# Four of eight row tiles transposed by VectorE in 32 by 32 blocks and two passes through memory

## The chip, the cores and the metric

The kernel runs on one core of a Trainium2 chip. A core has TensorE (matrix products, written PE in the profile), VectorE (DVE), ScalarE (ACT), GpSimd (POOL) and SyncE (SP), which issues most of the DMAs. Each runs its own instructions in order and waits for others by semaphores. SBUF is the working memory with 128 partitions; PSUM, eight banks of 128 x 512 float32, takes the matrix products. The metric is device time in microseconds, the median of several runs.

## The reference

One decoder layer on x of 1024 rows by 1024 columns, all in float32:

```python
h = rms_norm(x, norm_mix_g)
u = h @ w_in                                  # 1024 x 3328, split in five
y_pool = pool_mixer(u_pool, pool_w, pool_scale)
y_hgrn = hgrn2_mixer(q_raw, f_raw, i_raw, g_raw, lb, hgrn_norm_g)   # 6 heads
x = x + concat([y_pool, y_hgrn]) @ w_out
h2 = rms_norm(x, norm_mlp_g)
x = x + square(relu(h2 @ w_up)) @ w_down      # 1024 x 4096 and back
return rms_norm(x, final_norm_g)
```

The change lies between `w_out` and `w_up`, where h2 is made. A product on TensorE sums over the partitions of its operands. h2 comes out of the row norm with its rows on the partitions, and `h2 @ w_up` sums over its columns, so h2 has to be transposed.

## The kernel before

Rows are worked in NT = 8 tiles of P = 128 and columns in halves of 512. A float32 product is made of three: each operand is split into a high part, the value rounded to a shorter float (a cast on ScalarE, L126), and a low part, the rest (a subtraction on VectorE, L127). `mm3` (L132 to L134) then adds high by high, high by low and low by high. An operand is usable when both casts are done, and each split costs ScalarE and VectorE a pass over the data.

The stage around the change has these steps.

1. `product_out(i, 0)` makes the left half of x + mix @ w_out for tile i, 24 matmuls into one PSUM bank, for all eight tiles. `rows_out` adds x on VectorE (L828), squares on ScalarE with a sum (L880), and stores the half row with POOL's DMA (L881).
2. Then for each tile: the other half of its row of x is loaded by SP (L938), `product_out(i, 1)` makes the right half, and `rows_normed(i)` scales the row by 1/rms and the gain into `hn` (L887; the power is POOL's, L869).
3. `mlp_input(i - 1)` follows: eight transposes of 128 x 128 on TensorE (L893) into two banks, and two copies on ScalarE (L895) into `quad`. It runs one tile behind, so that TensorE need not wait for the norm. `quad[dh, h]` holds columns half dh (on the partitions, four blocks) of rows half h, 512 rows. Tiles 0 to 3 fill the two quarters `quad[0, 0]` and `quad[1, 0]`, tiles 4 to 7 the others.
4. `w_up` is multiplied by a seven-product scheme (Strassen-like): sums and differences of the quarters of h2 and of the weights go into products numbered 1 to 7. Operands 1 and 2 are the quarters of tiles 0 to 3, split in full after tile 4's product (`operand`). `mixed_blocks(i)` makes, for each of tiles 4 to 7, its part of operand 5 and the differences that become operands 6, 3, 7 and 4.
5. `up_product(n)` is 24 matmuls into two banks. Up group 0 has the order 1, 2, 5, 6, 3, 7, 4; the later groups start 1, 5, 6. Weights are loaded by SP (L958), summed or subtracted on VectorE, and split into `whi_wu` and `wlo_wu`.

On TensorE the order is that of the program. In front of up group 0, from `in_order.__enter__()` until the last operand of the group is made, it is written out for VectorE and ScalarE as well. Elsewhere a planner orders these two engines and SP by when it expects each instruction to be ready and by the place in the program. TensorE's order here is: right-half products 0 and 1, transposes of tile 0, product 2, transposes of tile 1, and so on to transposes of tile 6, up product 1, transposes of tile 7, up products 2, 5, 6, 3, 7, 4.

The pool `wsplit` has four buffers of each of two tags, `whi` and `wlo`. At the time of the change they pass from the four blocks of the left half of w_out to `hn_0`, `hn_1` and the x halves `xr_0`, `xr_1`, and to the first up weights.

The heads before this stage already use the helpers that the change calls. `blocks_turned` (L157) is one VectorE instruction that transposes each 32 x 32 block of a tile in place of the whole. `blocks_moved` writes the result to memory (L164) and reads it back in four DMAs (L167), one for each 32 partitions, so that every block lands on its partitions.

Of the kernel before, what the change touches and what calls it, by code (L numbers as in the profile page):

```python
# [10 lines left out]
F32 = mybir.dt.float32  # L11
# [6 lines left out]
P = 128  # L18
# [3 lines left out]
KT = D // P  # L22
# [43 lines left out]
def kernel(  # L66
# [20 lines left out]
    pe, act, dve, pool = nc.tensor, nc.scalar, nc.vector, nc.gpsimd  # L87
# [13 lines left out]
    def spill(shape, name):  # L101
        return dram.tile(shape, F32, name=name, tag=name)
# [50 lines left out]
    B = 32  # L153

    def blocks_turned(dst, src):

        dve.transpose(dst, src.rearrange("p n (b i) -> p b n i", i=B))  # L157

    def blocks_moved(dst, src, name):


        n = src.shape[2] * B
        t = spill([P, 4 * n], name)
        nc.sync.dma_start(t, src.rearrange("p b n i -> p (b n i)"))  # L164
        tv = t.rearrange("(a j) (b x) -> b j a x", a=4, b=4)
        for b in range(4):
            nc.sync.dma_start(dst[b * B:(b + 1) * B], tv[b])  # L167
# [7 lines left out]
    wring = {"raw": [], "split": [], "n": 0}  # L175
# [28 lines left out]
    with ExitStack() as pa:  # L204
# [474 lines left out]
        with tc.manual_schedule(engines={mybir.EngineType.PE, mybir.EngineType.DVE, mybir.EngineType.Activation}):  # L679
            for j in load_xt(0, (("Q", 2), ("Q", 2), ("K", 2), ("K", 2))):  # L680
# [5 lines left out]
                n = 1 if j < 2 else 2 if j % 2 == 0 else 0  # L686
# [103 lines left out]
        def bank(name):  # L790
            return psb.tile([P, 512], F32, tag="bank", name=name)
# [27 lines left out]
    def pair_of(pool_, name):  # L819

        t = pool_.tile([P, 2, 4, 512], F32R, tag="big", name=name)
        return t[:, 0], t[:, 1]
# [14 lines left out]
    with ExitStack() as pb:  # L837
# [4 lines left out]
        for n, (pool_, tag) in enumerate(((rawp, "raw"), (rawp, "raw"), (sums, "sum"), (sums, "sum"))):  # L842
            t = pool_.tile([P, 2, 512], F32, tag=tag, name=f"xl_{n}")
# [29 lines left out]
        quad = {k: quadp.tile([P, 4, 512], F32, tag="quad", name=f"quad_{k[0]}{k[1]}") for k in ((0, 1), (1, 0), (0, 0), (1, 1))}  # L873
# [9 lines left out]
        def rows_normed(i):  # L883
            r = rstd_of_parts([sss[i][:, e:e + 1] for e in range(2)], f"n2_{i}")
            for dh in range(2):
                cs = slice(dh * 512, (dh + 1) * 512)
                dve.scalar_tensor_tensor(out=hns[i][:, cs], in0=xs[i, dh], scalar=r, in1=g2[:, cs], op0=ALU.mult, op1=ALU.mult)  # L887

        def mlp_input(i):
            for dh in range(2):  # L890
                pt = bank(f"pt_h2_{i}_{dh}")
                for j in range(4):
                    pe.transpose(pt[:, j * P:(j + 1) * P], hns[i][:, (4 * dh + j) * P:(4 * dh + j + 1) * P], ident)  # L893
                c = i % 4 * P
                act.copy(quad[dh, i // 4][:, :, c:c + P], pt.rearrange("p (j t) -> p j t", j=4))  # L895
# [3 lines left out]
        def operand(n, pool_, src):  # L899
            h2[n] = pair_of(pool_, f"h2op_{n}")  # L900
            split(*h2[n], src)
# [7 lines left out]
        def mixed_blocks(i, between=lambda: None):  # L909


            b11, b12, b21, b22 = (quad[k][:, :, i % 4 * P:(i % 4 + 1) * P] for k in ((0, 0), (0, 1), (1, 0), (1, 1)))
            sub(b11, b12, b11)
            part = *(t[:, :, i % 4 * P:(i % 4 + 1) * P] for t in h2[5]), b11
            hi_part(*part)
            between()
            lo_part(*part)
            sub(b11, b22, b11)
            sub(b12, b22, b12)
            sub(b21, b21, b11)  # L920

        def product_out(i, dh):
            ps = bank(f"ps_o_{dh}_{i}")
            products_out({i: ps}, right_weight if dh else left_weight, MIX_ORDER)
            rows_out(i, dh, ps)
# [3 lines left out]
        for i in range(2, NT):  # L929
            product_out(i, 0)  # L930

        his = [wring["split"][0].tile([P, D], F32, tag="whi", name=f"hn_{n}") for n in range(2)]
        los = [wring["split"][0].tile([P, 2, 512], F32, tag="wlo", name=f"xr_{n}") for n in range(2)]
        hns = {i: his[i % 2] for i in range(NT)}
        for i in range(NT):
            xs[i, 1] = los[i % 4 // 2][:, i % 2]
        for i in range(NT):
            nc.sync.dma_start(xs[i, 1], x[0, i * P:(i + 1) * P, 512:])  # L938
            product_out(i, 1)
            rows_normed(i)  # L940
            if i:
                mlp_input(i - 1)
            if i == 4:
                operand(1, big, quad[0, 0])
                operand(2, big, quad[1, 0])
                h2[5] = pair_of(big2, "h2op_5")
            if i > 4:
                mixed_blocks(i - 1)
# [73 lines left out]
        for _ in up_product(1, split_first[1], first["a"], True):  # L1022
            pass
        mlp_input(7)
        made = {}
        mixed_blocks(7, lambda: made.update({6: first_weights(6)}))
# [121 lines left out]
    with ExitStack() as pd:  # L1148
# [116 lines left out]
        for at, (g, n) in enumerate(products[:-2]):  # L1265
            last = g == DOWN_GROUPS - 1
            pools, a, b = ahead
# [12 lines left out]
        with tc.manual_schedule(engines={mybir.EngineType.DVE, mybir.EngineType.Activation, mybir.EngineType.Pool}):  # L1280
            pools, a, b = ahead
# [84 lines left out]
```

## Time and profile before

| | |
|---|---|
| median of 3 runs | 1070.4 us (1070.05 to 1071.48) |
| the profiled execution | 1070.01 us |
| its span | 1068.2 us, 14588 instructions |
| DMA | 142.82 MB, mean 134 GB/s |

The span is the time from the first to the last instruction in the trace; all times of instructions count from its start. A timeline line has the start, the time, the engine, the line of the program, the operation, out<-in and the shapes, and in brackets how long the engine stood idle before and what released it. A matmul line's time includes the depth of TensorE's pipeline; the distance of two starts is what it takes. In the summary of one tile, three numbers with slashes are the shortest, the median and the longest time of an instruction, in ns.

### The profile page before, as it was taken

To read this page: it belongs to the slowest core of one execution; us is meant where nothing else is said; L and a number is where in the kernel's file an instruction comes from. 1 tells how busy PE (TensorE), PEld (TensorE's weight loads), DVE (VectorE), ACT (ScalarE), POOL (GpSimd) and SP (SyncE) were. 2 spreads that over 40 slices of the span, in tenths; PEclk is the share of its full clock that TensorE was granted. 3 is DMA by queue.
4 is the path that set the end of the run, shared out by engine and by line. 5 is a ranking of instruction groups with operands and counts; after the bars stand their busy time and mean duration, and the time that the engine had idled before them with its cause. 6 is when DMAs were issued, how large, how long until landed. Compare 5 with 4: busy or idle time off the path is not lost.

```text
span 1068.2 us, 14588 instructions
## 1 busy us (share of the span) xinstructions
PE 1056.5 (99%) x5890; PEld 885.5 (83%) x5890; DVE 748.0 (70%) x932; ACT 446.5 (42%) x720; POOL 78.3 (7%) x126
## 2 busy tenths in 40 slices
PE   9999999999999899999999999999999999999997
PEld 8988889988888688888888888888888888888886
DVE  5377686176588824798855865775979878777775
ACT  5856544354544523463223223323435242423334
POOL 0001000001000111101101100100100000000001
PEclk9999999999999999999999999999999999999999
DMA  9521121131111723225435434428983344254104
GB/s 307 176 61 55 56 70 40 59 93 49 39 40 41 246 104 114 70 99 179 174 104 193 178 109 148 178 99 323 375 344 119 116 160 175 101 202 153 39 1 158
DMA packets 74116, 142.82 MB, mean 134 GB/s; under 512 B 5440, under 2 KB 47168, under 8 KB 70464
## 3 DMA queue, kind: packets, MB, share of 16 engines
q1 hardware_dynamic: 63408, 106.32, 29.3%
q0 software_dynamic: 9344, 33.56, 8.0%
q10 hardware_dynamic: 1296, 2.00, 0.5%
q8 instruction: 46, 0.75, 0.3%
q14 instruction: 22, 0.18, 0.1%
HBM read 101.49 MB, written 40.37 MB: 133 GB/s over the span
## 4 chain that ended last, share of the span: by engine, by line
PE 96%; DVE 3%; issue 0%; POOL 0%; ACT 0%; POOLq 0%
PE ps_ua L134 5%; PE ps_ua L133 5%; PE ps_ua L132 5%; PE ps_dx L132 5%; PE ps_dx L133 5%; PE ps_dx L134 5%; PE ps_v L304 3%; PE ps_dy L132 3%; PE ps_uc L134 3%; PE ps_dy L133 3%; PE ps_uc L133 3%; PE ps_uc L132 3%; PE ps_dy L134 3%; PE ps_o L134 2%; PE ps_o L132 2%; PE ps_o L133 2%
## 5 line engine op out<-in xcount | busy, mean ns | idle before, releaser
L126 ACT CAST wdop<-raw_wd 128x2048 fp32r<-128x2048 f32 x28 | 53.6, 1913 | 156.1 <-PE ps_dy L134 49.6
L132 PE MATMUL ps_ua<-h2op,whi_wu 128*128 128x512 f32 x256 | 99.7, 389 | 0.0
L134 PE MATMUL ps_ua<-h2op,wlo_wu 128*128 128x512 f32 x256 | 99.6, 389 | 0.0
L133 PE MATMUL ps_ua<-h2op,whi_wu 128*128 128x512 f32 x256 | 99.6, 389 | 0.0
L132 PE MATMUL ps_dx<-wdop,hop 128*128 128x512 f32 x252 | 98.0, 389 | 0.0
L133 PE MATMUL ps_dx<-wdop,hop 128*128 128x512 f32 x252 | 98.0, 389 | 0.0
L134 PE MATMUL ps_dx<-wdop,hop 128*128 128x512 f32 x252 | 98.0, 389 | 0.0
L127 DVE TENSOR_TENSOR wdop<-raw_wd,wdop 128x2048 fp32r<-128x2048 f32 x28 | 64.1, 2290 | 29.3 <-ACT wdop L126 29.3
L126 ACT CAST hop<-hraw 128x2048 fp32r<-128x2048 f32 x28 | 53.4, 1911 | 31.6 <-DMA hraw<-hid 19.8
L127 DVE TENSOR_TENSOR hop<-hraw,hop 128x2048 fp32r<-128x2048 f32 x28 | 63.9, 2283 | 2.5 <-ACT hop L126 2.5
L126 ACT CAST whi_wu<-wsum 128x1024 fp32r<-128x1024 f32 x22 | 23.2, 1054 | 93.6 <-DVE wsum L825 38.7
L127 DVE TENSOR_TENSOR wlo_wu<-raw_wu,whi_wu 128x1024 fp32r<-128x1024 f32 x23 | 28.0, 1221 | 47.6 <-ACT whi_wu L126 47.6
L828 DVE TENSOR_TENSOR x<-ps_dx,x 128x512 f32<-128x512 f32 x64 | 43.8, 686 | 18.7 <-PE ps_dx L134 18.7
L133 PEld LDWEIGHTS ps_ua<-h2op,whi_wu 128*128 128x128 f32 x256 | 48.1, 188 | 10.0
L132 PEld LDWEIGHTS ps_ua<-h2op,whi_wu 128*128 128x128 f32 x256 | 48.1, 188 | 10.0
L134 PEld LDWEIGHTS ps_ua<-h2op,wlo_wu 128*128 128x128 f32 x256 | 48.1, 188 | 9.9
L134 PEld LDWEIGHTS ps_dx<-wdop,hop 128*128 128x128 f32 x252 | 47.3, 188 | 9.9
L132 PEld LDWEIGHTS ps_dx<-wdop,hop 128*128 128x128 f32 x252 | 47.3, 188 | 9.8
L133 PEld LDWEIGHTS ps_dx<-wdop,hop 128*128 128x128 f32 x252 | 47.3, 188 | 9.7
L1061 POOL DMA_DIRECT2D hid<-hid x56 | 29.9, 534 | 283.9 <-DVE hid L1058 216.9
L132 PE MATMUL ps_uc<-h2op,whi_wu 128*128 128x512 f32 x128 | 49.8, 389 | 0.0
L133 PE MATMUL ps_uc<-h2op,whi_wu 128*128 128x512 f32 x128 | 49.8, 389 | 0.0
(287 smaller groups left out, 2704.7 us busy)
## 6 DMA issues: line engine op xcount, KB each, us to landing
hid<-hid POOLq DMA_DIRECT2D x56, 512.0 KB, 3.2
hraw<-hid SPq DMA_DIRECT2D x28, 1024.0 KB, 5.1
raw_wu<-in_w_up_dram SPq DMA_DIRECT2D x32, 512.0 KB, 3.8
raw_wd<-in_w_down_dram SPq DMA_DIRECT2D x16, 1024.0 KB, 7.2
xt<-in_x_t_dram SPq DMA_DIRECT2D x16, 256.0 KB, 5.5
xn<-in_x_dram SPq DMA_DIRECT2D x8, 512.0 KB, 7.0
x<-x_mid SPq DMA_DIRECT2D x8, 512.0 KB, 6.1
raw_q<-in_w_in_dram SPq DMA_DIRECT2D x6, 512.0 KB, 4.4
```

Of the source, the lines that this page charges most:

```text
L126: act.copy(hi, src)
L127: dve.tensor_tensor(out=lo, in0=src, in1=hi.bitcast(F32), op=ALU.subtract)
L132: pe.matmul(ps, lh, rh, start=start, stop=False, skip_group_check=goes_on)
L133: pe.matmul(ps, lh, rl, start=False, stop=False, skip_group_check=goes_on)
L134: pe.matmul(ps, ll, rh, start=False, stop=stop, skip_group_check=goes_on)
L304: pe.matmul(banks[i][:, :VC], hT[h][part][:, j, i * P:(i + 1) * P], w[:, b, :], start=j == 0 and part == 0 and w is wh, stop=j == KT - 1 a ...
L828: dve.tensor_tensor(out=out_, in0=a, in1=b, op=ALU.add)
L1061: nc.gpsimd.dma_start(store[n][:, at, :], t)
```

## The change

For tiles 0 to 3 (`TURNED = 4`), `mlp_input` does without TensorE. VectorE turns the 32 x 32 blocks of the normalised tile into `turned`; SP writes that to memory and reads it back into `placed` in four DMAs; two copies on ScalarE put `placed` into the same places of `quad` as before. It is called right behind `rows_normed(i)` instead of one tile later. Tiles 4 to 7 go as before. `turned` and `placed`, two buffers each, are taken from the tags `whi` and `wlo` of `wsplit`, ahead of `hn` and `xr`.

```diff
+        TURNED = 4
+
         def mlp_input(i):
+            if i < TURNED:
+                t, n = placed[i % 2], turned[i % 2]
+                blocks_turned(n, hns[i].rearrange("p (n t) -> p n t", t=P))
+                blocks_moved(t.rearrange("p a n i -> p a (n i)"), n, f"h2_{i}")
+                c = i % 4 * P
+                for dh in range(2):
+                    dst = quad[dh, i // 4][:, :, c:c + P].rearrange("p j (a i) -> p j a i", i=B)
+                    act.copy(dst, t[:, :, 4 * dh:4 * dh + 4].rearrange("p a j i -> p j a i"))
+                return
             for dh in range(2):
...
+        turned = [wring["split"][0].tile([P, 4, KT, B], F32, tag="whi", name=f"h2_turned_{n}") for n in range(2)]
+        placed = [wring["split"][0].tile([P, 4, KT, B], F32, tag="wlo", name=f"h2_placed_{n}") for n in range(2)]
         his = [wring["split"][0].tile([P, D], F32, tag="whi", name=f"hn_{n}") for n in range(2)]
...
             rows_normed(i)
-            if i:
+            if i < TURNED:
+                mlp_input(i)
+            elif i > TURNED:
                 mlp_input(i - 1)
             if i == 4:
                 operand(1, big, quad[0, 0])
```

## The prediction

> **What bounds the kernel now.** First the busy shares and the chain of work that ended last, both on the page:
>
> ```profile
> PE 1056.5 (99%) x5890; PEld 885.5 (83%) x5890; DVE 748.0 (70%) x932; ACT 446.5 (42%) x720; POOL 78.3 (7%) x126
> PEclk9999999999999999999999999999999999999999
> PE 96%; DVE 3%; issue 0%; POOL 0%; ACT 0%; POOLq 0%
> ```
>
> TensorE bounds: 99% busy, full clock, 96% of the chain. An average says little about one stage, so next the busy time by stretch (us, then PE, PEld, DVE, ACT, POOL, clock, DMA share, GB/s):
>
> ```profile
> 406.00:434.00 28.00, 28.00 (x141) 23.54 (x140) 13.06 (x26) 10.38 (x21) 5.69 (x10) 1.00 0.37 123
> 434.00:461.00 27.00, 27.00 (x135) 22.37 (x135) 25.23 (x38) 12.63 (x22) 4.16 (x6) 1.00 0.13 49
> 461.00:495.00 34.00, 34.00 (x151) 28.16 (x150) 33.93 (x32) 17.79 (x19) 3.25 (x6) 1.00 0.40 137
> ```
>
> The transposes lie at 411 to 457. TensorE never stops there. VectorE is half idle up to 434 and then has no room: 25.2 of 27 and 33.9 of 34 us. So the second question is by how much VectorE is ahead of TensorE after 434. The timelines of both engines answer it:
>
> ```profile
> 434.82 4.50 DVE L127 TENSOR_TENSOR h2op<-quad,h2op 128x2048 fp32r<-128x2048 f32 x2
> 460.57 0.69 DVE L907 TENSOR_TENSOR h2op<-quad,h2op 128x512 fp32r<-128x512 f32 x1
> 462.61 0.39 PE L132 MATMUL ps_uc<-h2op,whi_wu 128*128 128x512 f32 x1
> 476.75 1.22 DVE L907 TENSOR_TENSOR wlo_wu<-wdif,whi_wu 128x1024 fp32r<-128x1024 f32 x1
> 478.93 0.39 PE L132 MATMUL ps_ua<-h2op,whi_wu 128*128 128x512 f32 x1
> 493.90 1.21 DVE L127 TENSOR_TENSOR wlo_wu<-wsum,whi_wu 128x1024 fp32r<-128x1024 f32 x1
> 495.25 0.39 PE L132 MATMUL ps_uc<-h2op,whi_wu 128*128 128x512 f32 x1
> ```
>
> Matmuls follow each other every 0.226 us (462.61 is the first of up product 5; 24 take 5.44). A product's second matmul needs the low part of its operand, its third that of its weights, whose load starts some 0.2 earlier. Product 5 of group 0 has its operand at 461.26 and needs it at 462.83: 1.6 us to spare. Product 7 has its weights at 477.97, needs them at 479.2: 1.2. Product 5 of group 1 has them at 495.11, needs them at 495.5: **0.4 us**. VectorE works without a break between these, so the stage is balanced to 0.4 us: whatever TensorE saves before it is kept only if VectorE's row of work moves earlier too.
>
> **The change part by part.** *Removed: 32 of 64 transposes.* Their group, the chain in order of time, and the additions on VectorE that follow each product:
>
> ```profile
> L893 PE MATMUL pt_h<-ident,hn x64: 270/272/328, 411.6 to 457.0; 128*128 128x128 f32 x64
> ...
> 411.56 0.23 PE ps_o L134
> 411.79 0.87 PE pt_h L893 x8
> 412.66 0.24 PE ps_o L132
> ...
> 400.94 0.69 DVE L828 TENSOR_TENSOR xl<-ps_o,xl 128x512 f32<-128x512 f32 x1 [4.75 <-PE ps_o L134]
> 406.38 0.69 DVE L828 TENSOR_TENSOR xr<-ps_o,xr 128x512 f32<-128x512 f32 x1 [4.75 <-PE ps_o L134]
> 424.53 0.69 DVE L828 TENSOR_TENSOR xr<-ps_o,xr 128x512 f32<-128x512 f32 x1 [1.99 <-PE ps_o L134]
> 430.86 0.69 DVE L828 TENSOR_TENSOR xr<-ps_o,xr 128x512 f32<-128x512 f32 x1 [2.33 <-PE ps_o L134]
> ```
>
> The matmuls overlap, so 8 x 0.272 isn't the price. A group of eight costs 0.87 to 0.9 us: the period is 6.33 with it, 5.44 without. Four groups: **3.6 us**, the most that can be won. Product 5 would start at 459.0.
>
> *Added: block transposes, a write, four reads per tile.* The kernel does the same for five heads, so this trace has the prices; the last two lines are SP's timeline for one head:
>
> ```profile
> L157 DVE STREAM_TRANSPOSE turned<-on x5: 1237/1245/1246, 109.2 to 306.5; 128x1024 f32<-128x1024 f32 x5
> DMA to landing us min/median/max: 2.6/2.6/4.5
> L167 SPq DMA_DIRECT2D onT<-on x20: 312/425/1707, 113.1 to 313.3; - x20
> DMA to landing us min/median/max: 2.4/2.9/5.0
> ...
> 263.05 0.34 SPq L164 DMA_DIRECT2D on<-turned  x1
> 265.74 2.08 SPq L167 DMA_DIRECT2D onT<-on  x4
> ```
>
> The first landing line is of the write, the second of the reads. VectorE: 4 x 1.245 = 5.0 us, all before 428, beside 15 us of idle: no cost. ScalarE makes as many copies of 128x512 as before, now out of SBUF, where its squares of that size (first row below) take 0.63 us against a copy's 0.58: nothing. What is new there is that a copy waits for reads, with the squares of later rows behind it, and behind these their normalisation; ScalarE is free for 18 of the 28 us, so a copy that comes in time costs nothing. SP issues 20 more DMAs and stands from a write to its landing: 2.7 + 2.1 = 4.8 of 5.44 us per tile. POOL's queue gets nothing. Behind SP's waits stand the x rows and weights:
>
> ```profile
> 412.75 0.63 ACT L880 ACTIVATE junk<-xr 128x512 bf16<-128x512 f32 x1
> 396.63 14.03 SPq L938 DMA_DIRECT2D xr<-in_x_dram  x5
> 427.90 0.38 SPq L958 DMA_DIRECT2D raw_wu<-in_w_up_dram  x1
> 449.51 1.22 DVE L828 TENSOR_TENSOR wsum<-raw_wu,raw_wu 128x1024 f32<-128x1024 f32 x1
> ```
>
> Four of the five x rows are wanted before the first write is ready, and can go first; their buffers now come free at the end of the left half's last product (added at 400.94), 4 us later, which leaves 5 us before 406.38. Later rows are loaded about 10 us ahead of their product's end, these weights 21.6 us before 449.51. No cost; if one were kept behind a write, 2.7 to 4.5 us of that margin would go.
>
> *Moved: when operand 1 can be made.* It needs all four tiles in the first half of `quad`, hence the fourth tile's transfers:
>
> ```profile
> 408.84 0.75 DVE L887 SCALAR_TENSOR_TENSOR hn<-xl,rstd_n,g 128x512 f32<-128x512 f32 x1 [0.69 <-POOL rstd_n L869]
> 409.51 0.75 DVE L887 SCALAR_TENSOR_TENSOR hn<-xr,rstd_n,g 128x512 f32<-128x512 f32 x1
> 432.40 0.58 ACT L895 COPY quad<-pt_h 128x512 f32<-128x512 f32 x1
> 432.87 3.73 ACT L126 CAST h2op<-quad 128x2048 fp32r<-128x2048 f32 x2
> ```
>
> Rows are normalised 3.9 us after their addition (406.38 to 410.26). The fourth is added at 406.38 + 3 x 5.44 = 422.7, normalised at 426.6, turned at 427.85; write issue to first read 2.7: 430.6; the fourth read issued 1.3 later, landed after 2.9: 434.8; two copies 1.1, a cast 1.9: VectorE begins operand 1 at **437.9**, against 434.82, so +3.1. With both maxima (4.5 and 5.0) it is 441.9, +7.1. I take 438.5, +3.7: nearer the medians, but not on them, since 512 KB of weights (427.90) and a row of x are issued right after the normalisation, beside this write.
>
> *Moved: two weight splits.* The new tiles take two of the four `whi`/`wlo` buffers, so the first two up weights wait for the copies of the third and fourth tile:
>
> ```profile
> 415.76 2.35 DVE L127 TENSOR_TENSOR wlo_wu<-raw_wu,whi_wu 128x1024 fp32r<-128x1024 f32 x2
> ```
>
> In before they lay in idle time. The first still finds a gap (431 to 437); the second, 1.17 us, may fall into the full stretch: 0 to 1.2, I take 0.6.
>
> *What VectorE gets back.* Row 5 is added at 433.6 and normalised before 437.5, ahead of operand 1 instead of behind it: 2.1 us. And it had these waits after 434:
>
> ```profile
> 442.44 0.75 DVE L887 SCALAR_TENSOR_TENSOR hn<-xl,rstd_n,g 128x512 f32<-128x512 f32 x1 [0.46 <-POOL rstd_n L869]
> 447.58 0.75 DVE L887 SCALAR_TENSOR_TENSOR hn<-xl,rstd_n,g 128x512 f32<-128x512 f32 x1 [0.46 <-POOL rstd_n L869]
> 453.96 0.75 DVE L887 SCALAR_TENSOR_TENSOR hn<-xl,rstd_n,g 128x512 f32<-128x512 f32 x1 [0.75 <-POOL rstd_n L869]
> ```
>
> 1.7 us together; with more work queued most are filled: 0.8 to 1.7, I take 1.2.
>
> **The sum.** VectorE's row of work moves by 3.7 + 0.6 - 2.1 - 1.2 = **+1.0 us** (ends: 3.1 + 0 - 2.1 - 1.7 = -0.7; 7.1 + 1.2 - 2.7, row 6 then being ahead as well, - 0.8 = +4.8). TensorE, 3.6 us early, runs into it at products 5 and 7, and last in group 1, where 0.4 us was to spare: the end moves by +1.0 - 0.4 = **+0.6 us** (-1.1 to +4.4). The 3.6 us are won and spent waiting. The profiled execution took 1070.01 us around its span of 1068.2, against a median of 1070.4; from the median: **1071.0 us**. A measurement of this kernel can tell about 0.2%, 2.1 us, from no change.
>
> **The rivals.** *Late transfers, slower.* Same mechanism, one place: the fourth tile's write and reads. It decides once they land 2.1 us later than by the medians (after 436.9): then operand 1 begins at 440.0, the row moves by 5.2 + 0.6 - 2.1 - 1.2 = 2.5 and the end by 2.1. For it: the maxima in the landing lines, SP's 4.8 of 5.44 us, and the squares behind ScalarE's waiting copies, which would delay the next tile's write. Against: medians of five heads, and a DMA share of 0.37. It gives 1072.5 to 1074.8, about 1073.5; chance 0.33.
>
> *VectorE's row does not bind, faster.* If the order on VectorE were made anew so that arithmetic on `hid` at 481 to 495 goes behind group 1's weights, TensorE would keep most of 3.6 us: 1066.8. Against: in group 0 that order is written by hand, and there product 5's operand, now ready at 461.26, would have to be ready by 459.2, though its source comes 3.1 us later. Chance 0.13.
>
> *The clock falls.* No slice shows a lower clock in this trace, whose longest wait of TensorE is
>
> ```profile
> PE ps_o L132 <- ACT mT_hi L126: 2.7, 1, 2.7
> ```
>
> If the waits, 3.6 + 4.4 us at the far end, came as one stop and a whole product ran at half rate after it, that adds 5.4 us: 1080. Chance 0.04. The Trainium skill, "TensorE: Matmul & The Clock Gate", section "Why this matters for your kernels", warns of gaps over about 3 us, after which the clock is halved; no run here shows one so long.
>
> The Trainium skill's "VectorE: DVE Perf Modes", section "Rules for kernel authors", also speaks against the change: a 128x128 transpose belongs on TensorE where its result may go to PSUM. By it alone there would be nothing to win, 1070.4 or more. The trace agrees that the detour is long, 434.8 - 426.6 = 8.2 us for turn, write and reads where TensorE's group takes 0.9.
>
> **How the numbers follow.** Balanced, so within 0.2%: 0.50, own range 1069.3 to 1072.5; late 0.33; faster 0.13; clock 0.04. Faster 0.13, same 0.50, slower 0.37. The range 1069.0 to 1075.0 leaves out the faster case and the clock's.
>
> **What would show it.** 32 transposes in the group of L893; additions 5.44 us apart up to 433.6; operand 1 on VectorE at about 438.5; TensorE waits of some 4 us in all between 440 and 500, for VectorE's `h2op`, `hn`, `wlo_wu`. No waits there and product 5 at 459 would make it wrong, as would x rows waiting behind writes on SP.

## The result, and the profile after

The kernel after takes **1089.06 us** (median of 4 runs, 1088.48 to 1089.51) against 1070.22 us for the kernel before in the same series, 18.8 us more. The ratio on record, 1.0166 with an interval of 1.0153 to 1.0179, makes it 17.8 us, a little less than these two medians do; where ratios are compared below, the loss is counted as 18 us. It is slower, where 1071.0 was forecast and 1075.0 was the upper end. The profiled execution took 1089.51 us around a span of 1087.7. One of the six timed runs of the kernel called e11 below took 6098.79 us and is left out of its time.

The page of the kernel after: TensorE's busy time, the clock that it was granted in 40 slices, and the chain that ended last.

```profile
PE 1060.2 (97%) x5858; PEld 886.7 (82%) x5858; DVE 752.8 (69%) x936; ACT 447.6 (41%) x720; POOL 77.5 (7%) x126
PEclk9999999999999899889999999999999999999999
PE 94%; DVE 3%; ACT 1%; issue 1%; DMA 1%; POOL 0%; SPq 0%; POOLq 0%; DVEq 0%; ACTq 0%
```

TensorE has 32 instructions fewer and is busy 3.7 us *longer*, and the clock row, all nines before, has three eights, at slices 14, 17 and 18. So there are two things to look for: stops, and matmuls that run slower. The waits of TensorE between 380 and 520 (us in total, times, longest); in the kernel before this view is empty:

```profile
PE pt_h L904 <- DVE hn L887: 8.2, 1, 8.2
PE ps_ua L132 <- ACT h2op L126: 5.1, 1, 5.1
PE ps_ua L133 <- DVE h2op L127: 1.5, 1, 1.5
```

Three waits, 14.8 us: one for a normalised row, two for operand 1. The first is followed back on VectorE, whose timeline has the additions of the right halves (L828) and operand 1's low part (L127):

```profile
415.61 0.69 DVE L828 TENSOR_TENSOR xr<-ps_o,xr 128x512 f32<-128x512 f32 x1 [0.29 <-PE ps_o L134]
...
431.93 1.29 DVE L828 TENSOR_TENSOR xr<-ps_o,xr 128x512 f32<-128x512 f32 x2 [11.15 <-PE ps_o L134]
437.37 1.29 DVE L828 TENSOR_TENSOR xr<-ps_o,xr 128x512 f32<-128x512 f32 x2 [4.15 <-PE ps_o L134]
...
465.98 4.49 DVE L127 TENSOR_TENSOR h2op<-quad,h2op 128x2048 fp32r<-128x2048 f32 x2 [0.62 <-ACT h2op L126]
```

The additions of rows 0 and 1 are 5.44 us apart (410.17, 415.61); then come rows 2 and 3 together, 16.3 us later. The bracket names TensorE, but `ps_o` of row 2 had been done since about 421, so it must have been the other operand, x. Why x was late, SP's timeline tells:

```profile
400.41 14.02 SPq L952 DMA_DIRECT2D xr<-in_x_dram  x3
415.35 0.33 SPq L164 DMA_DIRECT2D h<-h_turned  x1
418.21 1.75 SPq L167 DMA_DIRECT2D h_placed<-h  x4
420.80 0.34 SPq L164 DMA_DIRECT2D h<-h_turned  x1
421.25 1.60 SPq L952 DMA_DIRECT2D xr<-in_x_dram  x1
422.90 0.43 SPq L974 DMA_DIRECT2D raw_wu<-in_w_up_dram  x1
425.10 1.75 SPq L167 DMA_DIRECT2D h_placed<-h  x4
426.94 14.38 SPq L952 DMA_DIRECT2D xr<-in_x_dram  x3
```

Three x rows are issued first (0, 1 and 4); rows 2, 3 and 6 stand in the last line, behind the write and the reads of tile 1, and are issued from 426.94 on, 6 us after row 2's product was done. The buffers would explain it: rows 2 and 3 lie in `xr_1`, and `xr_0`, `xr_1` and both `placed` have the tag `wlo`.

The clock of this stretch, by windows of 3 us (PE busy, then PEld, DVE, ACT, POOL, clock, DMA share, GB/s):

```profile
443.00:446.00 3.00, 0.52 (x3) 0.52 (x4) 3.00 (x6) 0.89 (x1) 0.54 (x1) 0.50 0.84 269
446.00:449.00 3.00, 3.00 (x12) 2.66 (x11) 2.25 (x6) 1.32 (x3) 0.55 (x1) 0.53 1.05 269
...
466.00:469.00 3.00, 1.47 (x3) 0.86 (x4) 3.00 (x2) 1.74 (x1) 0.00 (x0) 0.50 0.20 74
469.00:472.00 3.00, 3.00 (x9) 2.32 (x8) 3.00 (x4) 0.89 (x2) 0.00 (x0) 0.50 0.00 0
```

Behind each of the two stops the clock is 0.50, and TensorE goes at about half rate: behind the second one its matmuls start 0.43 us apart instead of 0.226.

```profile
469.34 0.63 PE L132 MATMUL ps_ua<-h2op,whi_wu 128*128 128x512 f32 x1
469.77 0.63 PE L133 MATMUL ps_ua<-h2op,whi_wu 128*128 128x512 f32 x1
```

### The profile page after: what moved, and what is told of

Its sections match the earlier page's. It is cut to its first block, busy times and chain, and to the rows that moved or that the text cites. A ratio compares the mean times of both kernels' runs of the same rounds, so it can differ in the third digit from the quotient of the medians.

```text
span 1087.7 us, 14558 instructions
## 1 busy us (share of the span) xinstructions
PE 1060.2 (97%) x5858; PEld 886.7 (82%) x5858; DVE 752.8 (69%) x936; ACT 447.6 (41%) x720; POOL 77.5 (7%) x126
## 4 chain that ended last, share of the span: by engine, by line
PE 94%; DVE 3%; ACT 1%; issue 1%; DMA 1%; POOL 0%; SPq 0%; POOLq 0%; DVEq 0%; ACTq 0%
PE ps_ua L133 5%; PE ps_ua L132 5%; PE ps_ua L134 5%; PE ps_dx L134 5%; PE ps_dx L133 5%; PE ps_dx L132 5%; PE ps_v L304 3%; PE ps_dy L134 3%; PE ps_uc L132 3%; PE ps_dy L133 3%; PE ps_uc L134 3%; PE ps_uc L133 3%; PE ps_dy L132 3%; PE ps_o L132 3%; PE ps_o L133 2%; PE ps_o L134 2%
## 5 line engine op out<-in xcount | busy, mean ns | idle before, releaser
L132 PE MATMUL ps_ua<-h2op,whi_wu 128*128 128x512 f32 x256 | 100.8, 394 | 5.1 <-ACT h2op L126 5.1
L133 PE MATMUL ps_ua<-h2op,whi_wu 128*128 128x512 f32 x256 | 100.7, 393 | 1.5 <-DVE h2op L127 1.5
L127 DVE TENSOR_TENSOR wdop<-raw_wd,wdop 128x2048 fp32r<-128x2048 f32 x28 | 64.1, 2290 | 27.3 <-ACT wdop L126 27.3
L127 DVE TENSOR_TENSOR hop<-hraw,hop 128x2048 fp32r<-128x2048 f32 x28 | 63.9, 2283 | 3.2 <-ACT hop L126 3.2
L127 DVE TENSOR_TENSOR wlo_wu<-raw_wu,whi_wu 128x1024 fp32r<-128x1024 f32 x23 | 28.1, 1222 | 47.7 <-ACT whi_wu L126 47.6
L828 DVE TENSOR_TENSOR x<-ps_dx,x 128x512 f32<-128x512 f32 x64 | 43.9, 687 | 18.7 <-PE ps_dx L134 18.7
```

The costliest lines, as they stand in the source:

```text
L127: dve.tensor_tensor(out=lo, in0=src, in1=hi.bitcast(F32), op=ALU.subtract)
L132: pe.matmul(ps, lh, rh, start=start, stop=False, skip_group_check=goes_on)
L133: pe.matmul(ps, lh, rl, start=False, stop=False, skip_group_check=goes_on)
L828: dve.tensor_tensor(out=out_, in0=a, in1=b, op=ALU.add)
```

## The experiments

The theory after the result: the x rows behind tile 1's reads make the first stop, operand 1 is late for a reason of its own, and each stop is paid for again by the clock. The rivals: the pass through memory, or VectorE's turns, make all of it. Ratios are to the kernel before, timed on the same chip; 1.0010 is 1.07 us.

### x rows first in the program (e1), and buffers outside the tag (e2)

e1 moves the loads of rows 0 to 3 ahead in the program and leaves the buffers:

```diff
-        for i in range(NT):
+        for i in range(4):
             nc.sync.dma_start(xs[i, 1], x[0, i * P:(i + 1) * P, 512:])
+        for i in range(NT):
+            if i >= 4:
+                nc.sync.dma_start(xs[i, 1], x[0, i * P:(i + 1) * P, 512:])
```

> The change, with the loads of the first four x rows written ahead of the loop, so that they are planned before anything asks for the buffers of the blocks read back. Theory A (the x rows of tiles 2 and 3 share a tag with those buffers and are therefore issued behind the reads of tile 1; their lateness is nearly all of the 18.8 us): 1070 to 1074, no wait of TensorE for a normalised tile over 1 us, rows 2 and 3 added within 6 us of one another. Theory B (the way through memory itself is too slow, and the rows' order only a symptom): 1083 or more, with TensorE still waiting 5 us or more for operand 1.

e2 leaves the loads where they are in the program and takes `turned` and `placed` out of the shared tags, as views of fields of `quad` that tiles 4 to 7 fill later:

```diff
-        turned = [wring["split"][0].tile([P, 4, KT, B], F32, tag="whi", name=f"h2_turned_{n}") for n in range(2)]
-        placed = [wring["split"][0].tile([P, 4, KT, B], F32, tag="wlo", name=f"h2_placed_{n}") for n in range(2)]
+        def half_of(q, n, name):
+            return q[:, 2 * n:2 * n + 2, :].rearrange("p a (b i) -> p (a b i)", i=B).rearrange("p (a n i) -> p a n i", a=4, i=B)
+        turned = [half_of(quad[1, 1], n, "t") for n in range(2)]
+        placed = [half_of(quad[0, 1], n, "p") for n in range(2)]
```

> The change, with its four buffers laid into two quarters that nothing uses before tile 4, so that no tag is shared with the x rows or the weights; the loads stay where they were. Theory A: x rows 0 to 3 are issued together, and the time is that of e1 or up to 1 us less, since the first two weight splits move back too: 1069.5 to 1073. Theory B: 1083 or more. If the shared tag is not what orders the rows, rows 2 and 3 are late here as well, and the time is near 1089.

e1: 1077.67 us, 1.0055 (1.0043 to 1.0068). e2: 1077.42 us, 1.0054 (1.0041 to 1.0068). Two different edits, the same result: two thirds of the loss, 1.1% or 12 us, is gone, and the wait for the normalised row with it. e1's waits of TensorE:

```profile
PE ps_ua L132 <- ACT h2op L126: 4.2, 1, 4.2
PE ps_ua L133 <- DVE h2op L127: 1.6, 1, 1.6
PE ps_uc L133 <- DVE h2op L918: 0.9, 1, 0.9
PE ps_ua L132 <- ACT hid L1088: 0.4, 1, 0.4
```

So the rows were behind the reads because of both: the shared tag, and their later place in the program; taking away either is enough. Neither range of the expectations was met, for both theories were too simple: a third of the loss is left. Where it lies shows e2's timeline of SP:

```profile
396.90 14.01 SPq L955 DMA_DIRECT2D xr<-in_x_dram  x5
...
424.80 0.32 SPq L164 DMA_DIRECT2D h<-quad  x1
425.17 4.54 SPq L167 DMA_DIRECT2D quad<-h  x8
429.83 0.36 SPq L164 DMA_DIRECT2D h<-quad  x1
...
435.16 1.94 SPq L167 DMA_DIRECT2D quad<-h  x4
```

and of ScalarE:

```profile
447.34 0.63 ACT L880 ACTIVATE junk<-xr 128x512 bf16<-128x512 f32 x1 [5.04 <-DVE xr L828]
...
448.44 1.14 ACT L899 COPY quad<-quad 128x512 f32<-128x512 f32 x2
449.48 3.70 ACT L126 CAST h2op<-quad 128x2048 fp32r<-128x2048 f32 x2
```

All x rows go first. But tile 3's write, issued at 429.83, has landed only at 435.16, 5.3 us later, and its reads, of which the slowest took 5.3 us, are in at about 442. The planner has put the copies behind the square of row 7, so that they run at 448.44, and operand 1's low part begins at 451.47.

### The rows alone (e3)

All eight tiles are transposed by TensorE, one tile behind as before; turns, writes and reads of the first four are issued in the changed order, and nobody uses what they bring:

```diff
-                c = i % 4 * P
-                for dh in range(2):
-                    dst = quad[dh, i // 4][:, :, c:c + P].rearrange("p j (a i) -> p j a i", i=B)
-                    act.copy(dst, t[:, :, 4 * dh:4 * dh + 4].rearrange("p a j i -> p j a i"))
                 return
+
+        def mlp_input_pe(i):
...
-            elif i > TURNED:
-                mlp_input(i - 1)
+            if i:
+                mlp_input_pe(i - 1)
```

> All eight tiles transposed on TensorE one tile behind as before, and beside that, for four tiles, the turning, the write and the four reads of the change, whose result is not used (the copies out of it are left out). Theory A: the x rows are late as in the change, TensorE waits some 8 us or more for a normalised tile, and 3.6 us are not saved: 1080 to 1092. Theory B: nothing waits for the detour, 1070 to 1073.

1082.15 us, 1.0100 (1.0086 to 1.0113), in the first theory's range; the wait is a little under its 8 us. TensorE's waits, and VectorE's addition of rows 2 and 3:

```profile
PE pt_h L902 <- DVE hn L887: 6.9, 2, 6.7
```

```profile
429.06 1.29 DVE L828 TENSOR_TENSOR xr<-ps_o,xr 128x512 f32<-128x512 f32 x2 [10.32 <-DMA xr<-in_x_dram]
```

Here the bracket names the load of x itself. No operand depends on the pass, and there is no wait for one; the wait for the normalised row stays. The late rows alone are enough for 1%.

### Without turns and pass (e4), with two tiles (e7), without the pass (e8)

e4, against the kernel after:

```diff
-                t, n = placed[i % 2], turned[i % 2]
-                blocks_turned(n, hns[i].rearrange("p (n t) -> p n t", t=P))
-                blocks_moved(t.rearrange("p a n i -> p a (n i)"), n, f"h2_{i}")
...
-                    act.copy(dst, t[:, :, 4 * dh:4 * dh + 4].rearrange("p a j i -> p j a i"))
+                    act.copy(quad[dh, i // 4][:, :, c:c + P], hns[i].rearrange("p (h j t) -> p h j t", h=2, j=4)[:, dh])
```

> The four tiles are copied into the quarters as they are: their transposition is left out. It is the most that taking 32 transposes off TensorE can bring. If a group of eight costs 0.9 us and the following stage can use it: 1066.3 to 1067.5. If VectorE's row of work or anything else stops TensorE anyway: 1068.5 to 1070.5.

e4: 1070.51 us, 0.9993 (0.9984 to 1.0002). The 32 transposes are gone and nothing has been put in their place, and the time is that of before, at the upper end of the second range. TensorE's wait, and the two windows behind it:

```profile
PE pt_h L900 <- DVE hn L887: 1.7, 1, 1.7
```

```profile
437.00:440.00 3.00, 2.99 (x14) 2.33 (x13) 2.42 (x6) 2.30 (x5) 0.85 (x2) 0.68 0.23 86
440.00:443.00 3.00, 3.00 (x11) 2.36 (x11) 2.68 (x4) 0.00 (x0) 0.28 (x1) 0.75 0.02 4
```

TensorE, ahead of VectorE, stops 1.7 us for row 4, and then has the lower clock for a while.

e7 is e2 with two tiles turned:

```diff
-        TURNED = 4
+        TURNED = 2
```

> e2 with two tiles instead of four by the way through memory; tiles 2 and 3 transposed on TensorE. The last transposed tile then comes off TensorE, so operand 1 doesn't wait for memory. Theory C and the prediction's row of work: 1.8 us off TensorE, half of it kept at most: 1069.5 to 1072. If the 1 MB of writes and reads cost anything by themselves (DMA or SP held up): 1073 or more.

1071.07 us, 1.0002 (0.9994 to 1.0011): nothing won and nothing lost; the only wait is 0.8 us for a normalised row.

e8 is e2 without the pass; the copies read `turned`:

```diff
-                blocks_moved(t.rearrange("p a n i -> p a (n i)"), n, f"h2_{i}")
-                    act.copy(dst, t[:, :, 4 * dh:4 * dh + 4].rearrange("p a j i -> p j a i"))
+                    act.copy(dst, n[:, :, 4 * dh:4 * dh + 4].rearrange("p a j i -> p j a i"))
```

> e2 without the pass through memory: the copies read the blocks as VectorE left them, which leaves out putting them on their partitions. It keeps VectorE's four turns of 1.245 us. If these are hidden, as the prediction has it: within 1 us of e4, 1070 to 1071.5. If VectorE has no room for them: 1073 or more.

1075.1 us, 1.0039 (1.0026 to 1.0053). This lies in the second theory's range, but what stops TensorE is an order and not the length of the turns: the planner now took operands 1 and 2 ahead of row 4 on VectorE (operand 1's low part from 434.41, row 4's norm at 439.57), and TensorE stood for that row:

```profile
PE pt_h L903 <- DVE hn L887: 5.4, 1, 5.4
```

So no cost of the turns can be read from e8. The planner's orders differ from kernel to kernel, and each of e2, e4 and e8 has one of its own.

### Orders written by hand (e5, e6, e9 to e13)

To compare parts at the same order, VectorE, ScalarE and SP were ordered by hand over the right-half products. In e5, and in e6, where SP was left to the planner, the copies of tile i stand behind the reads of tile i + 2 into the same buffer, so the fields hold another tile's rows and each copy waits a pass longer; they took 1087.79 us, 1.0161 (1.0147 to 1.0175), and 1089.19 us, 1.0171 (1.0157 to 1.0185), and leave their question open.

> e2, with the order of SP, ScalarE and VectorE written by hand over right-half products 0 to 5: on SP each tile's write, reads and one later x row, on ScalarE the copies of tile i behind the squares of tile i + 2. Theory C (in e2 the transfers are not what is slow: SP lets reads stand behind the next tile's write, and ScalarE lets the copies of tile 3 stand behind the squares of tile 7): operand 1 begins on VectorE at 438 to 442 instead of 451.5, the time is 1069.5 to 1073.5. Theory D (memory is slow under this load, write and reads over 5 us each): operand 1 after 445, 1075 or more.

> e5, with SP left to the planner: reads of tile 1 again behind the write of tile 2, the write of tile 3 behind two x rows and 1 MB of weights. If ScalarE's order was the cost in e2: within 1 us of e5. If SP's order was: 2 us or more above e5, near e2's 1077. Theory D: as e5 and e2.

e9 has the copies of tile i (`received`) ahead of tile i + 2's turn, write and reads (`sent`), with e2's buffers:

```diff
+        with tc.manual_schedule(engines={mybir.EngineType.DVE, mybir.EngineType.Activation, mybir.EngineType.SP}):
+            for i in range(4):
+                row_load(i)
+            for i in range(NT):
+                product_out(i, 1)
+                if 2 <= i < 6:
+                    received(i - 2)
...
+                rows_normed(i)
+                if i < TURNED:
+                    sent(i)
+                    row_load(i + 4)
+                if i > 4:
+                    mlp_input(i - 1)
+                if i == 5:
+                    operand(1, big, quad[0, 0])
...
```

> The change with the two buffers as views of the second operand's fields (as in the run before with ratio 1.0054), and with the order of VectorE, ScalarE and SyncE's queue over the right half's products written out by hand: the first four x rows ahead, each tile's reads right behind its write's wait with one row or weight piece between them, the copies of tile i on ScalarE behind the square of row i+2, operand 1 behind row 5. Theory C: what was left there, some 7 us, was the planner's order (write 2 ahead of reads 1, tile 3's copies behind the square of row 7): operand 1's low part then begins on VectorE at 438 to 442 and not at 451, TensorE's waits for it fall under 2 us, no window of 3 us shows a clock under 0.8 between 440 and 470, and the time is 1069.5 to 1073.5. Theory D: the passes through memory themselves are late, since their writes and reads take 5 us each beside the weights and not 2.6 and 2.9: operand 1's low part begins after 445 whatever the order, TensorE waits 3 us or more for it, and the time is 1075 or more.

e10 has neither turns nor pass, as e4, and each tile's copies behind its norm. e11 is the kernel before. These two share an order that is written out up to product 5 only:

```diff
+            for i in range(6):
+                product_out(i, 1)
+                rows_normed(i)
+                if i < 4:
+                    row_load(i + 4)
+                if i:
+                    mlp_input(i - 1)
+            operand(1, big, quad[0, 0])
+            operand(2, big, quad[1, 0])
```

> The first four tiles copied into the operand's fields without being transposed, no pass through memory (leaves out the transposition of these four tiles), with the order of the same three engines written out by hand up to product 5: the most that taking 32 transposes off TensorE can bring here. If only the planner's order kept the saving from showing in the run that did this without a hand order (1.7 us of waiting for the normalised tile): 1066.5 to 1068. If the stage is balanced, so that VectorE or the weights bound it once TensorE's 3.6 us go: 1069 to 1070.7, with new waits of TensorE of 2 us or more between 430 and 500.

> The kernel before with the same three engines' order written out by hand up to product 5: the control for the two above. If the hand order is worth nothing by itself: within 1 us of the kernel before. If it is worth something: 2 us or more to either side, which would then have to be taken off both.

e13 is e9 with the turns alone, in e9's order, which runs through all eight products and has each tile's copies two tiles later:

```diff
-            blocks_moved(t.rearrange("p a n i -> p a (n i)"), n, f"h2_{i}")
...
-            t, c = placed[i % 2], i % 4 * P
+            t, c = turned[i % 2], i % 4 * P
```

> The hand-written order (ratio 1.0061), with VectorE's four turns but without the pass through memory: the copies read the turned tile itself (leaves the blocks on the wrong partitions, and leaves out the four writes and sixteen reads). If the pass is what makes the 6.9 us between the hand order with everything (1077.57) and the one with neither turns nor pass (1070.64): operand 1's low part begins on VectorE before 440, TensorE waits under 3 us in all, 1070 to 1072. If VectorE's 5 us of turns make them: operand 1 later than 441, TensorE waits 4 us or more, 1074.5 to 1078.

| | us | ratio, interval |
|---|---|---|
| e11: 64 transposes on TensorE | 1074.30 | 1.0032 (1.0020 to 1.0044) |
| e10: e11 with 32 of them left out | 1070.64 | 0.9996 (0.9987 to 1.0005) |
| e13: four turns, e9's order | 1072.81 | 1.0017 (1.0008 to 1.0026) |
| e9: e13 with the pass | 1077.57 | 1.0061 (1.0048 to 1.0073) |

The shorter order by hand costs 0.3% by itself, the control's second case. So only kernels of one order can be compared: 32 transposes fewer (e11 to e10) are worth -0.36%, 3.7 us between the medians; the pass (e13 to e9) costs +0.44%, 4.7 us. From e10 to e13 it is +0.21%, 2.2 us, for the turns and the other order together; no run tells these two apart. From e10 to e9, then, 6.9 us are lost, where the transposes save 3.7.

e13's 1072.81 lies between its two ranges. Its operand 1, at 441.01, is on the edge of the second; less the 2.1 us by which this execution is late at the left half's last addition it is 438.9, inside the first. Its waits, 3.0 us, are on the first's edge. So the pass makes most of the 6.9 us, but not all.

e9 was to tell whether the planner's order or the pass itself held up e2's operand. SP's write and first read of tile 3 in e9:

```profile
432.12 0.38 SPq L164 DMA_DIRECT2D h<-quad  x1
...
438.34 1.74 SPq L167 DMA_DIRECT2D quad<-h  x4
```

ScalarE's copies of that tile:

```profile
442.88 1.14 ACT L900 COPY quad<-quad 128x512 f32<-128x512 f32 x2 [4.55 <-DMA quad<-h]
```

VectorE's operand 1, and TensorE's waits:

```profile
446.83 2.29 DVE L127 TENSOR_TENSOR h2op<-quad,h2op 128x2048 fp32r<-128x2048 f32 x1 [5.01 <-ACT h2op L126]
```

```profile
PE pt_h L906 <- DVE hn L887: 8.7, 2, 7.5
```

Now ScalarE waits for the data, not for its order. The operand comes after 445 and the time is over 1075, as the theory of the slow pass had it; only, TensorE stops for normalised rows and not for the operand. The order by hand begins operand 1 some 5 us earlier than e2 does (446.83 against 451.47) and gains nothing: here row 6's addition stands behind operand 1, and TensorE waits for that row.

### What makes the pass slow (e12), and what stands behind the operand (e14)

e12 is e9 with two weight pieces of 512 KB issued behind the last reads instead of between the passes:

```diff
+                if i == 3:
+                    for dk in range(2):
+                        w_first[1, dk] = up_raw(0, 1, dk, rawp)
```

> The change in the hand-written order (ratio 1.0061), with one edit: the two weight pieces of 512 KB that SyncE's queue issued between the passes through memory (419.35 and 428.51) are issued behind the reads of the fourth tile. Theory D1, the passes are late because these pieces share the DMA engines with them (pass 1 beside nothing: write landed in 2.7 us; passes 2 to 4 beside pieces and rows: writes in 4.2, 4.3 and 6.2 us): the writes of tiles 1 to 3 then land in under 3.5 us, ScalarE's copies of tile 2 wait under 2 us (4.75 before), operand 1's low part begins on VectorE at 438 to 441.5 (446.83), TensorE's waits for the normalised tile fall from 8.7 us under 5, and the time is 1070.5 to 1074. Theory D2, the passes are late by their own traffic and by the rows written and read beside them: writes of 4 us or more, operand 1 after 445, TensorE's waits of 7 us or more, and 1076 to 1078.5.

1077.12 us, 1.0059 (1.0045 to 1.0072): the time is in the second theory's range, and operand 1, at 445.75, as well, while TensorE's wait of 6.6 us and two of the writes lie between the two theories. Tile 3's write and reads on SP, and its copies on ScalarE:

```profile
431.85 0.38 SPq L164 DMA_DIRECT2D h<-quad  x1
...
436.58 1.78 SPq L167 DMA_DIRECT2D quad<-h  x4
```

```profile
441.80 1.14 ACT L900 COPY quad<-quad 128x512 f32<-128x512 f32 x2 [5.56 <-DMA quad<-h]
```

The writes of tiles 0 to 3 had landed after 2.7, 3.9, 3.9 and 4.7 us; in e9 it was 2.7, 4.2, 4.3 and 6.2. The pieces account for up to 1.5 us of the last write; without them a write still takes a good microsecond more than the first, beside the x rows, the half rows that POOL stores, and the passes' own traffic. Which of these it is was not tried. The reads of tile 3 didn't get faster but slower, 3.3 to 3.8 us against 2.6 to 3.1 in e9: the pieces, issued at 438.87, now ran beside them.

e14 is e9 with row 6 and tile 4's copies ahead of tile 3's copies and of operand 1:

```diff
-                if 2 <= i < 6:
+                if 2 <= i < 5:
                     received(i - 2)
...
-                if i == 5:
+                if i == 6:
+                    received(3)
                     operand(1, big, quad[0, 0])
```

> The hand-written order with everything (ratio 1.0061), with one edit: row 6's addition, square and normalisation and tile 4's copies stand ahead of the last tile's copies and of operand 1 on VectorE and ScalarE. If the late data (copies of the last tile at 442 to 443) stop TensorE only through what is queued behind operand 1 (row 6, 8.7 us of waiting for the normalised tile): that wait falls under 2 us, a wait for operand 1 of at most 3 us takes its place, no half clock after it, 1070.5 to 1073.5. If the late operand stops TensorE by itself: waits for operand 1 and 2 of 4 us or more in its place, 1075 or more.

1077.41 us, 1.0061 (1.0048 to 1.0073): the second theory's time, without its wait of 4 us for the operand. Tile 4's copies go here into fields in which part of tile 3's blocks still lay, so this part of the output holds other values, and ScalarE stood for the reads before these copies too.

```profile
PE pt_h L906 <- DVE hn L887: 3.6, 1, 3.6
PE ps_ua L133 <- DVE h2op L127: 1.8, 1, 1.8
PE ps_ua L132 <- ACT h2op L126: 0.5, 1, 0.5
```

5.1 us of the 8.7 are gone, 2.3 come back as a wait for the operand, and the time is the same: what matmuls took longer, as reckoned below, rises from 1.8 to 3.6 us. Whether an order could hide the late data is neither shown nor excluded, since row 6's square stood behind copies that waited for it.

## Why the prediction was wrong, step by step

One sum holds all of it. From the left half's last addition (400.94 before, 404.73 after) to the end of the span, the profiled executions take longer than the kernel before by the first column. Take off TensorE's waits behind that point and add the transposes saved, at 0.9 us a tile; the rest is what matmuls took longer (all in us):

| | longer | waits | saved | rest |
|---|---|---|---|---|
| after | 15.7 | 14.8 | 3.6 | 4.5 |
| e1 | 6.1 | 7.1 | 3.6 | 2.6 |
| e2 | 6.0 | 6.8 | 3.6 | 2.8 |
| e3 | 10.6 | 6.9 | 0 | 3.7 |
| e4 | -0.1 | 1.7 | 3.6 | 1.8 |
| e9 | 6.9 | 8.7 | 3.6 | 1.8 |
| e10 | -0.5 | 2.3 | 3.6 | 0.8 |
| e11 | 4.3 | 2.4 | 0 | 1.9 |
| e13 | 1.7 | 3.0 | 3.6 | 2.3 |

Most of the rest belongs to the windows with a lower clock: in e11 the stretch 452 to 458, at clock 0.72, has 20 instructions in 5.45 us of busy time, where at least 24 would go at 0.226 us. Not all of it does: e10's clock is 1.00 in every window of 3 us from 428 to 479, and it has a rest of 0.8. So the column is good to about 1 us.

*"Four of the five x rows are wanted before the first write is ready, and can go first … No cost."* **This step failed**, and it made the largest part: e1 and e2 take back 12 of the 18 us. That they can go first was true, and e1 does it; that they do was taken for granted, not read from the program. (The 4 us by which they were to go out later did not come: the first is issued 4.3 us ahead of the left half's last addition in both kernels.) Rows 2 and 3 share a tag with `placed`, whose buffers come first in the program. The price named for a row kept behind a write, 2.7 to 4.5 us of a margin, was too small as well: row 2 wasn't behind one write but behind two, two sets of reads, a row and a weight piece, and VectorE added it 16.3 us after row 1.

*Operand 1 on VectorE at 438.5.* This step failed as well, and the third of the loss that e1 and e2 leave hangs on it. Wrong by 7.4 us even in e9, where the rows go first and the order is given: 446.83, less the 0.9 by which that execution is late at 401. By the terms of the sum: the turn 1.7 us late (429.18), SP with the write another 1.7 (432.12, behind tile 2's reads and a row), the write 6.2 instead of 2.7, the reads 4.5 instead of 1.3 + 2.9, copies and cast 3.95 instead of 3.0; of these 8.1 us, 0.6 was allowed for. The term that was furthest off is the write, by 3.5 us: the medians came from the heads, and the first write here, with little beside it, took just as long, 2.7 us; the fourth did not.

*The rival of the late transfers* had the right mechanism and place, and its point of decision, 436.9, was passed by some 5 us. Its price of 1072.5 to 1074.8 was too low: it let VectorE's row of work slip by a few us, and counted neither TensorE's stop in front of the operand or of row 6 nor the clock behind it.

*The clock, chance 0.04.* It was priced for one stop at the far end; every kernel with a wait of 5 us or more has a clock of about 0.50 behind it, and the rest column of those in the table is 1.8 to 4.5 us. The Trainium skill, "TensorE: Matmul & The Clock Gate", section "Why this matters for your kernels", names gaps over about 3 us; the trace agrees, with 0.50 behind the stops of 8.2 and 5.1 us. But e4's clock fell to 0.68 behind a stop of 1.7 us, so here the measurement decides: the figure is no bound below which a stop is safe.

*3.6 us to win, and the stage balanced.* Both held in size. At one order the transposes are worth 3.7 us (e10 against e11), though the agreement is partly luck: in the two profiled executions some 1 us of the difference is in the rest column, because e11's clock fell behind its stop and e10's did not. In the planner's order e4 keeps nothing that can be measured: 1.7 us go into a wait for row 4 and 1.8 into the rest. But the place was not the forecast one (products 5, 7 and group 1's 5). It was row 4's norm, before them, so the reckoning of what each product has to spare was not what decided.

*Turns "no cost".* Four at 1.25 us, as forecast. That they cost nothing is not shown: e13 lies 2.2 us above e10, of which 0.7 is a longer wait for the normalised row and 1.5 stand in the rest column, but the two differ in their order too.

What stays open: why the later writes take longer, and why the planner puts a load that shares a tag behind the reads. And after's profile was already 3.8 us late at the left half's last addition, 2.6 of them from the program part at 366 to 373 that the change doesn't touch (below). How many of its timed runs had this is not known. No kernel here that computes the whole layer beats the one before.

## What to carry to other kernels

Where new buffers take a tag in common with tiles that are loaded ahead, read the order of first use in the program: a load can end up behind a write and a read that nothing in the data puts ahead of it. A latency measured where a transfer is alone is a lower bound; count what else is issued in the same microseconds before it goes into a sum whose margin is 2 us. And price a stop of TensorE twice, as the wait and as the lower clock behind it.

## What the runs showed of the hardware

The clock doesn't fall at a fixed length of stop. Two stops for `pt_h` by almost the same time, e10's and then e11's on TensorE's timeline, each with one of some 0.6 us behind it:

```profile
449.25 0.66 PE L900 MATMUL pt_h<-ident,hn 128*128 128x128 f32 x4 [1.69 <-DVE hn L887]
```

```profile
451.59 0.63 PE L893 MATMUL pt_h<-ident,hn 128*128 128x128 f32 x4 [1.81 <-DVE hn L887]
```

and the windows behind them, in the same order:

```profile
451.00:454.00 3.00, 3.00 (x16) 2.46 (x15) 3.00 (x7) 2.26 (x4) 0.58 (x1) 1.00 0.03 5
```

```profile
452.00:458.00 6.00, 5.45 (x20) 4.29 (x19) 5.58 (x11) 3.46 (x6) 1.98 (x2) 0.72 0.12 44
```

The one kept the full clock, then and in the windows up to 479; the other didn't. And at 364, in a part that is the same in every kernel, all executions have waits of 2.7 and 1.0 us; behind them the clock stays full in some and falls in others. Before, then after:

```profile
366.00:373.00 7.00, 6.67 (x28) 5.23 (x29) 5.14 (x8) 3.74 (x7) 0.78 (x2) 1.00 1.04 370
```

```profile
366.00:373.00 7.00, 5.48 (x13) 4.32 (x14) 5.95 (x9) 3.83 (x6) 0.76 (x1) 0.56 1.03 362
```

From the end of the wait of 2.7 us to the left half's last addition it takes 34.6 us in the four profiled executions with the full clock (before, e2, e9, e11), 35.7 to 36.3 in the eleven with 0.76 or 0.77, and 37.2 in after's. The same stop is thus free in one execution and costs 1.1 to 2.6 us in another, where the kernel before's timed runs spread over 2.1 us in one series (1069.72 to 1071.81). A write of 512 KB from SBUF to memory landed after 2.7 us with little beside it and after 6.2 us beside rows and weights, in a stretch (e9, 430 to 440) in which the DMA engines were 0.77 busy.
